# Output projection of a hybrid decoder layer as seven half-size products, its weight sums made by adding transfers

## The chip, the cores and the metric

One core of one Trainium2 chip. The metric is the device time of one execution of the whole layer in microseconds, as the median of several runs. TensorE (PE) does the matrix products, ScalarE (ACT) the casts and activations, VectorE (DVE) the elementwise work, GpSimd (POOL) a few scalings and a DMA queue of its own, SyncE (SP) the other DMA queue. Tiles live in SBUF, results of TensorE in banks of PSUM.

## The reference

One decoder layer in fp32 with batch 1, 512 tokens, D = 1024 and an FFN of width 2816. Three attention branches (sliding window, stick-breaking, cross-attention to a memory of 256 rows) are gated and merged; then:

```python
merged = (g[:, :, 0] * jnp.einsum('bse,ed->bsd', y_swa, w_branch_swa[l])
          + g[:, :, 1] * jnp.einsum('bse,ed->bsd', y_sb, w_branch_sb[l])
          + g[:, :, 2] * jnp.einsum('bse,ed->bsd', y_mem, w_branch_mem[l]))
mix = jnp.einsum('bsd,de->bse', merged, w_out[l])
h = h + rms_norm(mix, ln_mix_post[l])
u = rms_norm(h, ln_ffn_pre[l])
a = jax.nn.silu(jnp.einsum('bsd,df->bsf', u, w_gate[l])) * jnp.einsum('bsd,df->bsf', u, w_up[l])
ffn = jnp.einsum('bsf,fd->bsd', a, w_down[l])
h = h + rms_norm(ffn, ln_ffn_post[l])
```

The change is in `mix`: 512 x 1024 by 1024 x 1024.

## The kernel before

Every fp32 product is done as three products of fp32r parts (`mm3`, L167): high by high, high by low, low by high. `split` (L132) makes the parts: ScalarE casts the high part (L135), VectorE subtracts it from the source for the low part (L136). Weights come as 512 KB loads of 128 x 1024 on SyncE's queue and are split; activations are split where they are made.

Two streams (`Stream`, L33) lay out the work: `dn` runs the projections, gates and branches, `fs` the FFN. Each unit has a load, a split and its products; `run(us)` and `until(flag)` emit pieces of a stream, so that other code can be written in between. A stream's loads are emitted some units ahead of its products. Within an engine, instructions run in the order in which they stand; a framework sets the waits between engines. Blocks under `tc.high_priority()` may be moved up.

Buffers: `ckp` has 68 tiles of 128 x 512; `wp` holds the first stage's weights (`raw` 5, `hi` 4, `lo` 4 tiles of 128 x 1024) and is closed by `first.close()`; the FFN's pool `fp` is opened behind it in the same space, so that its first loads wait for whoever last read the space.

The last stages of `dn` are the gates of the MEM branch (`add_quarters`) and its four units of `branch` (L583): each product br is multiplied by its gate (L593), added to the sum of the other branches (L601), and the merged tile c (128 features x 512 tokens) is split into `mgh`, `mgl`. While the branch runs, eight loads of `w_out` and sixteen 512-wide splits are emitted (`out_load`, `out_split`).

`mix(t)` (L1051), for the four token tiles, does 2 output halves x 8 feature tiles x 3 products of 128 x 512 into two banks `mx`, 192 products in all. Then comes a chain of two norms: squares on ScalarE with a row sum (L1060), `rstd_small` (L1032: small operations, b and v, t and r, that go between VectorE and ScalarE), the gain (VectorE L1063), the residual `xr` (L1064), squares again (L1065), `rstd_small`, the gain (L1068) into the tiles `mt`. `turn(t)` (L1110) transposes `mt` on TensorE into `ut` (L1114) and makes the FFN's left factors: for t = 0, 1 the parts `B11`, `B21` (L1102, L1103) and copies `ur` (L1120); for t = 2, 3 `T1` and, later, `N2`, `N22`, `T3`, `T4`, from `ut` and `ur`. The FFN's products `gx`, `gw`, `gy` use these; gate, up and down are already done by seven products for eight, with weight sums of which some are made by adding transfers on GpSimd's queue (L1173). The first products of the program come behind nine warm-up products (`WARM`).

Of the kernel before, what the change touches and what calls it, by code (L numbers as in the profile page):

```python
# [103 lines left out]
def tile_kernel(ctx, tc, a):  # L104
# [913 lines left out]
    wo = {}  # L1018

    def out_load(h, q):  # L1020
        src = a["w_out"][:, h, 2 * q : 2 * q + 2].rearrange("p k n -> p (k n)")
        st[("wo", h, q)] = w_load(src, 1024)

    def out_split(h, q):
        raw = st.pop(("wo", h, q))
        for i in range(2):
            k = 2 * q + i
            wh, wl = ck(f"woh{h}{k}", F32R), ck(f"wol{h}{k}", F32R)
            split(raw[:, i * 512 : (i + 1) * 512], wh[:, :], wl[:, :])
            wo[(h, k)] = (wh[:, :], wl[:, :])  # L1030
# [380 lines left out]
    for i, (h, q) in enumerate(outs):
        out_load(h, q)
        out_split(h, q)
        dn.run(2.5)
# [188 lines left out]
```

## Time and profile before

| | |
|---|---|
| runs | 794.35, 794.44, 798.24 us |
| median | 794.44 us |
| profiled execution | 793.57 us, its span 791.8 us, granted clock 0.999 |

The profile is that of one execution. The page gives each engine's busy time as a share of the span, and the chain of work that ended last, followed back from the last instruction. The timeline of an engine has the start, the duration, engine, line, operation, output<-inputs, count, and in brackets the idle time before it with what ended it. The windows give each engine's busy time (and the number of its instructions) in stretches of the span, then TensorE's granted clock, the DMA engines' share and GB/s. Products are pipelined: 0.39 is how long one is in flight, and the distance of two starts is what one costs. Names are those of the program without buffer numbers.

### The profile page before, as it was taken

Reading aid. Unit: us, or ns where it says so; the run is one execution under the profiler, and the core shown is the slowest. Engines: PE = TensorE matmul, PEld = TensorE weight load, DVE = VectorE, ACT = ScalarE, POOL = GpSimd, SP = SyncE. Lnnn points to the kernel's source line nnn. Section 1 sums busy time; section 2 is a strip of 40 time slices with the busy share of each in tenths; the row PEclk is TensorE's granted clock in tenths of the full one; section 3 lists DMA queues with packets and bytes.
Section 4 is the critical chain, followed back from the end, with each engine's and each line's share of the span. In section 5 each row is a group of like instructions: output and inputs, shape, how many; then the busy total and the mean of one; then the engine's idle time right before and its main releaser. Section 6 shows DMA issues by size and latency. Waiting matters only on the chain.

```text
span 791.8 us, 12739 instructions
## 1 busy us (share of the span) xinstructions
PE 782.6 (99%) x4873; PEld 696.7 (88%) x4873; DVE 617.2 (78%) x960; ACT 454.8 (57%) x834; POOL 79.9 (10%) x103
## 2 busy tenths in 40 slices
PE   9999999999999999999999999999999999999996
PEld 6899887877888889889988899999999999888885
DVE  6998977754677796996694689868677767898797
ACT  7566755643664554765644477544445555666573
POOL 1101201000000001000013100010000000215200
PEclk9999999999999999999999999999999999999999
DMA  8443346122232308325769808877677751959802
GB/s 300 139 150 107 118 161 213 53 79 82 81 80 78 84 4 239 77 56 158 237 211 334 175 27 244 236 213 192 180 186 187 185 153 51 209 124 232 195 1 106
DMA packets 41870, 117.55 MB, mean 148 GB/s; under 512 B 4656, under 2 KB 6592, under 8 KB 41808
## 3 DMA queue, kind: packets, MB, share of 16 engines
q1 hardware_dynamic: 31872, 87.71, 34.1%
q0 software_dynamic: 9648, 28.82, 19.5%
q8 instruction: 38, 0.62, 0.3%
q14 instruction: 24, 0.20, 0.1%
q10 hardware_dynamic: 288, 0.20, 0.1%
HBM read 113.05 MB, written 3.67 MB: 147 GB/s over the span
## 4 chain that ended last, share of the span: by engine, by line
PE 95%; DVE 2%; issue 1%; DMA 0%; ACT 0%; SPq 0%; DVEq 0%
PE gx L172 5%; PE gx L169 5%; PE gx L171 5%; PE g L169 3%; PE br L169 3%; PE g L172 3%; PE br L171 3%; PE g L171 3%; PE br L172 3%; PE x L171 3%; PE x L172 3%; PE x L169 3%; PE gy L172 2%; PE gy L171 2%; PE gy L169 2%; PE mx L171 2%
## 5 line engine op out<-in xcount | busy, mean ns | idle before, releaser
L135 ACT CAST hi<-gw 128x1024 fp32r<-128x1024 f32 x77 | 79.8, 1048 | 81.7 <-DVE gw L1191 40.4
L136 DVE TENSOR_TENSOR lo<-gw,hi 128x1024 fp32r<-128x1024 f32 x77 | 93.6, 1223 | 34.0 <-ACT hi L135 33.9
L135 ACT CAST hi<-raw 128x1024 fp32r<-128x1024 f32 (+2 forms) x52 | 53.8, 1040 | 52.8 <-PE g L171 13.7
L136 DVE TENSOR_TENSOR lo<-raw,hi 128x1024 fp32r<-128x1024 f32 (+2 forms) x52 | 62.9, 1213 | 21.0 <-ACT hi L135 20.8
L1173 POOL DMA_DIRECT2D gw<-in_w_gu x27 | 23.3, 893 | 190.2 <-DMA gw<-in_w_gu 117.2
L135 ACT CAST hi<-r 128x1024 fp32r<-128x1024 f32 (+1 forms) x24 | 23.6, 982 | 19.9 <-PE y L172 5.3
L171 PE MATMUL x<-lo,lh 128*128 128x512 f32 x88 | 34.2, 389 | 0.0
L169 PE MATMUL x<-hi,lh 128*128 128x512 f32 x88 | 34.2, 389 | 0.0
L172 PE MATMUL x<-hi,ll 128*128 128x512 f32 x88 | 34.1, 389 | 0.0
L825 DVE TENSOR_TENSOR_SCAN p<-r,anew 128x512 f32<-128x512 f32 (+1 forms) x24 | 24.7, 1040 | 8.1 <-ACT r L189 7.6
L136 DVE TENSOR_TENSOR lo<-r,hi 128x1024 fp32r<-128x1024 f32 (+1 forms) x24 | 27.1, 1130 | 3.7 <-ACT hi L135 3.6
L136 DVE TENSOR_TENSOR lo<-qw,hi 128x1024 fp32r<-128x1024 f32 x18 | 21.9, 1219 | 8.9 <-ACT hi L135 8.9
L135 ACT CAST hi<-qw 128x1024 fp32r<-128x1024 f32 x18 | 18.9, 1050 | 15.8 <-PE g L171 3.7
L135 ACT CAST hi<-bp 128x512 fp32r<-128x512 f32 x33 | 19.1, 620 | 13.4 <-PE y L172 4.8
L136 DVE TENSOR_TENSOR lo<-bp,hi 128x512 fp32r<-128x512 f32 x33 | 22.2, 708 | 5.4 <-ACT hi L135 5.1
L172 PE MATMUL gx<-N2h,lo 128*128 128x256 f32 x88 | 25.0, 284 | 0.3 <-DVE lo L136 0.3
L169 PE MATMUL gx<-B11h,hi 128*128 128x256 f32 x88 | 25.1, 285 | 0.2 <-ACT B11h L1102 0.2
L172 PE MATMUL gw<-B21h,lo 128*128 128x256 f32 x88 | 25.0, 284 | 0.0
L169 PE MATMUL mx<-woh,mgh 128*128 128x512 f32 x64 | 25.0, 390 | 0.0
L171 PE MATMUL gx<-B11l,hi 128*128 128x256 f32 x88 | 25.0, 284 | 0.0
L172 PE MATMUL mx<-woh,mgl 128*128 128x512 f32 x64 | 24.9, 389 | 0.0
L172 PE MATMUL gy<-T1h,lo 128*128 128x256 f32 x88 | 24.9, 283 | 0.0
(910 smaller groups left out, 2900.8 us busy)
## 6 DMA issues: line engine op xcount, KB each, us to landing
gw<-in_w_gu SPq DMA_DIRECT2D x57, 512.0 KB, 5.0
gw<-in_w_gu POOLq DMA_DIRECT2D x27, 512.0 KB, 6.8
raw<-in_w_p SPq DMA_DIRECT2D x26, 512.0 KB, 4.2
qw<-in_w_p SPq DMA_DIRECT2D x15, 512.0 KB, 4.2
raw<-in_w_br SPq DMA_DIRECT2D x12, 512.0 KB, 3.8
bp<-in_w_dn SPq DMA_DIRECT2D x22, 256.0 KB, 8.4
r<-in_w_dn POOLq DMA_DIRECT2D x10, 512.0 KB, 8.2
raw<-in_w_out SPq DMA_DIRECT2D x8, 512.0 KB, 4.4
```

Of the source, the lines that this page charges most:

```text
L135: ins = nc.scalar.copy(hi, raw)
L136: lows = nc.vector.tensor_tensor(lo, raw, hi.bitcast(F32), op=ALU.subtract)
L169: one = nc.tensor.matmul(out, lh, rh, start=start, stop=False, skip_group_check=True)
L171: nc.tensor.matmul(out, *two, start=False, stop=False, skip_group_check=True)
L172: st["product"] = nc.tensor.matmul(out, *three, start=False, stop=stop, skip_group_check=True)
L825: ins = nc.vector.tensor_tensor_scan(p[:, :w], left1[i][:, :w], anew[:, o : o + w], 0.0, op0=ALU.mult, op1=ALU.max)
L1173: nc.gpsimd.dma_start(gw[(n, key)][:, :], g_src(n, i, j), accum_op=ALU.add)
```

## The change

`w_out` and `merged` are each seen as 2 x 2 blocks (feature half by output half; feature half by token half), and the product of blocks is done with seven half-size products p1 to p7 instead of eight. Each is 2 token tiles x 4 feature tiles x 3 products of 128 x 512: 168 products instead of 192.

- Weights: the sums of blocks of `w_out` are made in place: 12 plain loads of 256 KB (`wo_raw`, SyncE) and 16 transfers that add (`wo_plus`, GpSimd's queue), with 28 splits of 512 (`wo_split`). A tile is split for one product, then added to, then split for the next. The factors of p6 and p3 take four `hi`/`lo` pairs of `wp`.
- Left factors: made in the merged tiles in `branch` and in `turned_s`, `turned_r`, `turned_q`, `turned_d`, by 256-wide differences and sums and 256-wide splits.
- Results: p1, p5, p6 are copied from PSUM (ScalarE); p2, p3 and p7 are added to or subtracted from the copies (VectorE joins). `mix(0)` and `mix(1)` read such copies; `mix(2)` and `mix(3)` read the bank behind p4 and the join of p7. The norms of `mix` are as before, ten lines or so further down per line number (squares L1122 and L1127, gains L1125, residual L1126, L1130; turn's casts L1164, L1165, L1182, transposes L1176; FFN loads L1232, adding ones L1235).
- Places: the weights' loads start in the middle of the MEM gates (`dn.mark("half")`); `first.close()`, and with it `fp`, comes behind p3(1) instead of ahead of the first mix; `turn(0)` and `turn(1)` stand between the last products; `WARM` is 11.

```diff
-WARM = 9
+WARM = 11
...
-                h, l = ck(f"mgh{c}", F32R), ck(f"mgl{c}", F32R)
-                split(acc[:, :], h[:, :], l[:, :])
-                merged[c] = (h, l)
+                merged[c] = acc
+                if c < 4:
+                    if c % 2 == 0:
+                        ma.append((ck(f"mah{c}", F32R), ck(f"mal{c}", F32R)))
+                    sl = slice((c % 2) * 256, (c % 2) * 256 + 256)
+                    split(acc[:, :256], ma[-1][0][:, sl], ma[-1][1][:, sl])
+                    continue
+                mbd.append(parts(f"mbd{c}", acc))
+                nc.vector.tensor_tensor(acc[:, 256:], merged[c - 4][:, 256:], acc[:, 256:], op=ALU.subtract)
...
+    def wo_raw(key, j, h):
+        wsum[key] = [ck(f"wo{key}{k}") for k in range(4)]
+        for k, t in enumerate(wsum[key]):
+            nc.sync.dma_start(t[:, :], a["w_out"][:, h, 4 * j + k])
+
+    def wo_plus(key, j, h):
+        for k, t in enumerate(wsum[key]):
+            nc.gpsimd.dma_start(t[:, :], a["w_out"][:, h, 4 * j + k], accum_op=ALU.add)
...
+        if p not in ("p6", "p3"):
+            hl = tuple(ck(f"wo{p}{x}{k}", F32R)[:, :] for x in "hl")
+        else:
+            if k % 2 == 0:
+                uid[0] += 1
+                st["wo_two"] = [wp.tile([P, 1024], F32R, tag=x, name=f"{x}{uid[0]}", bufs=4) for x in ("hi", "lo")]
+            hl = tuple(x[:, (k % 2) * 512 : (k % 2) * 512 + 512] for x in st["wo_two"])
...
+    def turned_q(k):
+        lo, hi = merged[k], merged[4 + k]
+        nc.vector.tensor_tensor(hi[:, :256], lo[:, :256], hi[:, :256], op=ALU.add)
+        split(hi[:, :256], *(x[:, :256] for x in mqs[k]))
...
+    MIX = dict(p1="x", p6="x", p7="x", p4="x", p5="y", p3="y", p2="w")
...
+        with tc.high_priority():
+            if p in ("p1", "p5", "p6"):
+                t = mkeep[(p, i)] = ck(f"mk{p}{i}")
+                nc.scalar.copy(t[:, :], ps[:, :])
+            elif p == "p2":
+                t = mkeep[("p1", i)]
+                nc.vector.tensor_tensor(t[:, :], ps[:, :], t[:, :], op=ALU.add)
+            elif p == "p3":
+                t = mkeep[("p6", i)]
+                nc.vector.tensor_tensor(t[:, :], ps[:, :], t[:, :], op=ALU.subtract)
+            elif p == "p7":
+                t = mkeep[("p5", i)]
+                nc.vector.tensor_tensor(t[:, :], t[:, :], ps[:, :], op=ALU.subtract)
...
     def mix(t):
...
-            mm3(ps[h][:, :], (merged[k][0][:, tok], merged[k][1][:, tok]), wo[(h, k)], k == 0, k == KC - 1)
+        ps = (mkeep[("p1", i)], mkeep[("p6", i)]) if t < 2 else (mbank[("x", i)], mkeep[("p5", i)])
...
     dn.until(f"branch{MEM}")
+    for i in range(2):
+        mix_mm("p1", i)
...
+    mix_mm("p5", 0)
+    mix_mm("p6", 0)
+    for k in range(4):
+        wo_split("p7", "b", k)
+        turned_d(k)
+    mix_mm("p3", 0)
+    table("natural_log_exp_and_others")
+    tmp[0] = mix(0)
+    for k in range(4):
+        wo_split("p4", "r", k)
+    for p in ("p5", "p6", "p3"):
+        mix_mm(p, 1)
     first.close()
...
     fs.ahead(2, -1)
     tmp[1] = mix(1)
     fs.ahead(4, 0)
+    mix_mm("p7", 0)
+    turn(0, tmp[0])
+    mix_mm("p4", 0)
     tmp[2] = mix(2)
-    turn(0, tmp[0])
     fs.ahead(5, 3)
+    mix_mm("p7", 1)
+    turn(1, tmp[1])
+    mix_mm("p4", 1)
     tmp[3] = mix(3)
-    turn(1, tmp[1])
```

The order of the instructions at three places, before and after. First VectorE, around the first norm: `mkp60` is the kept copy of p6 for token tile 0, `mkp50` that of p5, `wop4l` are lows of p4's weights, `ssm0` the row sums of mix(0)'s squares, `mt0` and `xr0` its tiles. Before:

```order
L136 TENSOR_TENSOR mgl6_4366<-g16_2044,mgh6_4365 128x512
L136 TENSOR_TENSOR mgl7_4413<-g17_2077,mgh7_4412 128x512
L1036 TENSOR_SCALAR b_m0_4478<-ssm0_4472 128x1
L1038 SCALAR_TENSOR_TENSOR v_m0_4479<-ssm0_4472,b_m0_4478 128x1
L1040 SCALAR_TENSOR_TENSOR t_m0_4480<-r_m0_4481,v_m0_4479 128x1
L1041 SCALAR_TENSOR_TENSOR r_m0_4481<-t_m0_4480,r_m0_4481 128x1
L1063 SCALAR_TENSOR_TENSOR mt00_4474<-mx00_4422,r_m0_4481,bc_g_post0_4395 128x512
L1063 SCALAR_TENSOR_TENSOR mt01_4475<-mx01_4423,r_m0_4481,bc_g_post1_4396 128x512
L1064 TENSOR_TENSOR xr00_4379<-xr00_4379,mt00_4474 128x512
L1064 TENSOR_TENSOR xr01_4380<-xr01_4380,mt01_4475 128x512
```

And after:

```order
L136 TENSOR_TENSOR wop7l3_4608<-wob3_4193,wop7h3_4607 128x512
L1110 TENSOR_TENSOR mkp60_4587<-my0_4560,mkp60_4587 128x512
L1051 TENSOR_SCALAR b_m0_4633<-ssm0_4627 128x1
L1053 SCALAR_TENSOR_TENSOR v_m0_4634<-ssm0_4627,b_m0_4633 128x1
L136 TENSOR_TENSOR wop4l0_4662<-wor0_3921,wop4h0_4661 128x512
L136 TENSOR_TENSOR wop4l1_4666<-wor1_3922,wop4h1_4665 128x512
L1055 SCALAR_TENSOR_TENSOR t_m0_4635<-r_m0_4636,v_m0_4634 128x1
L136 TENSOR_TENSOR wop4l2_4670<-wor2_3923,wop4h2_4669 128x512
L1056 SCALAR_TENSOR_TENSOR r_m0_4636<-t_m0_4635,r_m0_4636 128x1
L136 TENSOR_TENSOR wop4l3_4674<-wor3_3924,wop4h3_4673 128x512
L1113 TENSOR_TENSOR mkp50_4573<-mkp50_4573,mx0_4418 128x512
L1125 SCALAR_TENSOR_TENSOR mt00_4629<-mkp10_4431,r_m0_4636,bc_g_post0_4306 128x512
```

Ahead of the first norm's small operations now stands a join, among them four weight lows, and behind them another join, which is of p7(0).

Second, ScalarE, around the squares of mix(2) and mix(3): `ut00` is the transposed tile of turn(0), `ut10` that of turn(1), `hi158` the high part of an FFN weight. Before, up to the squares of mix(3):

```order
L1060 ACTIVATE mt20_4673,ssm2_4671<-mx20_4621 128x512
L1060 ACTIVATE mt21_4674,ssm2_4671<-mx21_4622 128x512
L1102 CAST B11h0_3611<-ut00_4705 128x2x128
L189 ACTIVATE t_m2_4679<-ssm2_4671,b_m2_4677 128x1
L189 ACTIVATE r_m2_4680<-t_m2_4679 128x1
L1102 CAST B11h1_3613<-ut00_4705 128x2x128
L1065 ACTIVATE mt20_4673,ssh2_4672<-xr20_4387 128x512
L1065 ACTIVATE mt21_4674,ssh2_4672<-xr21_4388 128x512
L1120 COPY ur00_4715<-ut00_4705 128x512
L189 ACTIVATE t_h2_4695<-ssh2_4672,b_h2_4693 128x1
L1102 CAST B21h0_3615<-ut01_4706 128x2x128
L189 ACTIVATE r_h2_4696<-t_h2_4695 128x1
```

After, the squares of mix(2) and what stands ahead of them:

```order
L1164 CAST B21h1_3619<-ut01_4803 128x2x128
L1164 CAST B11h0_3613<-ut10_4896 128x2x128
L135 CAST hi158_4879<-gw152_4778 128x1024
L1182 COPY ur01_4813<-ut01_4803 128x512
L1122 ACTIVATE mt20_4838,ssm2_4836<-mx0_4418 128x512
L1122 ACTIVATE mt21_4839,ssm2_4836<-mkp50_4573 128x512
L1164 CAST B21h0_3617<-ut11_4897 128x2x128
L189 ACTIVATE t_m2_4844<-ssm2_4836,b_m2_4842 128x1
```

The squares of mix(2) stood ahead of turn(0)'s casts; now they stand behind the first of turn(1)'s and an FFN cast. And after, the squares of mix(3):

```order
L1182 COPY ur11_4907<-ut11_4897 128x512
L1127 ACTIVATE mt20_4838,ssh2_4837<-xr20_4496 128x512
L1127 ACTIVATE mt21_4839,ssh2_4837<-xr21_4497 128x512
L189 ACTIVATE t_h2_4860<-ssh2_4837,b_h2_4858 128x1
L189 ACTIVATE r_h2_4861<-t_h2_4860 128x1
L1122 ACTIVATE mt30_4932,ssm3_4930<-mx1_4433 128x512
L1122 ACTIVATE mt31_4933,ssm3_4930<-mkp51_4690 128x512
```

They stand behind `r_h2`, the end of mix(2)'s second norm, and behind all of turn(1)'s casts and copies. Before, they also stood behind `r_h2`, but ahead of all of turn(1)'s, with `B21h1` and `ur01` of turn(0) between.

Third, TensorE, from the last product of the mix to the first of the FFN: `ut10`, `ut11` are turn(1)'s transposes, `ut20` those of turn(2). Before:

```order
L169 MATMUL mx31_4741<-woh17_4356,mgh7_4412 128x512
L171 MATMUL mx31_4741<-wol17_4357,mgh7_4412 128x512
L172 MATMUL mx31_4741<-woh17_4356,mgl7_4413 128x512
L1114 MATMUL ut10_4824<-c_ident_364,mt10_4570 128x128 x4
L1114 MATMUL ut11_4825<-c_ident_364,mt11_4571 128x128 x4
L169 MATMUL gx0_4847<-B11h0_3611,hi159_4617 128x256
L1114 MATMUL ut20_4874<-c_ident_364,mt20_4673 128x128 x4
L171 MATMUL gx0_4847<-B11l0_3612,hi159_4617 128x256
```

And after:

```order
L169 MATMUL mx1_4433<-wop4h3_4673,mbd7h_4413 128x512
L171 MATMUL mx1_4433<-wop4l3_4674,mbd7h_4413 128x512
L172 MATMUL mx1_4433<-wop4h3_4673,mbd7l_4414 128x512
L1176 MATMUL ut10_4896<-c_ident_366,mt10_4738 128x128 x4
L1176 MATMUL ut11_4897<-c_ident_366,mt11_4739 128x128 x4
L169 MATMUL gx0_4965<-B11h0_3613,hi155_4785 128x256
L171 MATMUL gx0_4965<-B11l0_3614,hi155_4785 128x256
L172 MATMUL gx0_4965<-B11h0_3613,lo155_4786 128x256
```

Turn(1)'s transposes still follow the last product; turn(2)'s first stands later, behind more of the FFN's products.

More of the change, by code (lines that the diff above doesn't have):

```diff
@@ L579, in mem_vals @@
         return gen
-    merged = [None] * 8
+    merged, ma, mbd = [None] * 8, [], []
     def branch(b, c2, order):
@@ L634, in tile_kernel @@
             add_quarters(b, 0)
+            dn.mark("half")
             add_quarters(b, 1)
@@ L1016, in bcast, with wo_split @@
         return t
[L1018 to L1030, printed above, removed]
+    wsum, wt = {}, {}
+    def wo_raw(key, j, h):
[5 more added lines that the diff above has]
+            nc.gpsimd.dma_start(t[:, :], a["w_out"][:, h, 4 * j + k], accum_op=ALU.add)
+    def wo_split(p, key, k):
+        if p not in ("p6", "p3"):
[5 more added lines that the diff above has]
+            hl = tuple(x[:, (k % 2) * 512 : (k % 2) * 512 + 512] for x in st["wo_two"])
+        split(wsum[key][k][:, :], *hl)
+        wt[(p, k)] = hl
     def rstd_small(name, ss):
@@ L1049, in x_load, with turned_s, turned_r @@
             nc.sync.dma_start(hres[t][h][:, :], a["x"][t * P : (t + 1) * P, h * 512 : (h + 1) * 512])
+    mqs, mrd = [], []
+    mbank, mkeep = {}, {}
+    def turned_s(k):
+        mqs.append((ck(f"mqh{k}", F32R), ck(f"mql{k}", F32R)))
+        split(merged[4 + k][:, 256:], *(x[:, 256:] for x in mqs[k]))
+    def turned_r(k):
+        lo, hi = merged[k], merged[4 + k]
+        mrd.append((ck(f"mrh{k}", F32R), ck(f"mrl{k}", F32R)))
+        nc.vector.tensor_tensor(lo[:, 256:], lo[:, :256], lo[:, 256:], op=ALU.subtract)
+        nc.vector.tensor_tensor(lo[:, :256], hi[:, 256:], lo[:, :256], op=ALU.subtract)
+        split(lo[:, :256], *(x[:, :256] for x in mrd[k]))
@@ L1406, in down @@
         return gen
-    outs = [(h, q) for h in range(2) for q in range(4)]
-    dn.until(f"gates{MEM}")
[L1411 to L1414, printed above, removed]
+    dn.until("half")
+    wo_raw("r", 0, 0)
+    wo_raw("b2", 1, 0)
+    dn.run(4.0)
+    for k in range(4):
+        wo_split("p1", "r", k)
+        dn.run(2.0)
+    wo_plus("r", 0, 1)
+    dn.until(f"gates{MEM}")
+    wo_raw("b", 1, 1)
+    for k in range(4):
+        wo_split("p2", "b2", k)
+        dn.run(1.3)
+    for k in range(4):
+        wo_split("p5", "r", k)
+        dn.run(1.3)
+    wo_plus("r", 1, 1)
+    gpost = bcast("g_post")
+    gfpre = bcast("g_fpre")
+    for k in range(4):
+        wo_split("p3", "b", k)
+        dn.run(1.3)
+    wo_plus("b", 0, 1)
+    dn.until(f"branch{MEM}")
+    for i in range(2):
+        mix_mm("p1", i)
+    for k in range(4):
+        turned_s(k)
+    for k in range(4):
+        turned_r(k)
     for t in range(NT):
         x_load(t)
-    gpost = bcast("g_post")
-    gfpre = bcast("g_fpre")
-    dn.until(f"branch{MEM}")
+    for k in range(4):
+        wo_split("p6", "r", k)
+    wo_plus("r", 1, 0)
+    for i in range(2):
+        mix_mm("p2", i)
+    for k in range(4):
+        turned_q(k)
+    tmp = {}
+    mix_mm("p5", 0)
+    mix_mm("p6", 0)
+    for k in range(4):
+        wo_split("p7", "b", k)
[3 more added lines that the diff above has]
+    tmp[0] = mix(0)
+    for k in range(4):
+        wo_split("p4", "r", k)
+    for p in ("p5", "p6", "p3"):
+        mix_mm(p, 1)
     first.close()
```

20 lines of the change are left out of this document (14 added, 6 removed).

## The prediction

> **What bounds the kernel now.** I read the page first: the busy shares, then the chain that ended last.
>
> ```profile
> span 791.8 us, 12739 instructions
> PE 782.6 (99%) x4873; PEld 696.7 (88%) x4873; DVE 617.2 (78%) x960; ACT 454.8 (57%) x834; POOL 79.9 (10%) x103
> ...
> PE 95%; DVE 2%; issue 1%; DMA 0%; ACT 0%; SPq 0%; DVEq 0%
> ```
>
> TensorE is busy all the way and 95% of the last chain is its own work, so a product taken away is worth its full spacing as long as nothing else becomes late. The table of windows shows how much room the other engines have around the output projection: the branch stretch and the first half of the mix, the part of the mix in which VectorE had nothing to do, the norms, and the first FFN block.
>
> ```profile
> core 0: us, PE busy (x) PEld busy (x) DVE busy (x) ACT busy (x) POOL busy (x), PEclk, DMA share, GB/s
> 392.00:432.70 40.70, 40.70 (x181) 33.72 (x180) 29.64 (x52) 18.25 (x38) 9.12 (x7) 1.00 0.86 271
> 415.65:424.34 8.69, 8.69 (x40) 7.20 (x39) 0.00 (x0) 0.00 (x0) 5.05 (x6) 1.00 1.02 407
> 424.34:463.40 39.06, 38.89 (x210) 33.44 (x209) 28.37 (x69) 24.25 (x67) 6.02 (x7) 1.00 0.75 168
> 463.40:485.70 22.30, 22.00 (x185) 21.80 (x184) 21.47 (x38) 15.24 (x31) 1.72 (x2) 1.00 0.46 119
> ```
>
> VectorE is the second engine here: idle for 8.69 us, then 28.37 of 39.06, then 21.47 of 22.30, which is full. The TensorE timeline (start, duration) says how that last stretch meets the products.
>
> ```profile
> 410.31 0.39 PE L169 MATMUL mx<-woh,mgh 128*128 128x512 f32 x1
> ...
> 437.74 0.39 PE L171 MATMUL mx<-wol,mgh 128*128 128x512 f32 x1
> ...
> 484.62 0.39 PE L172 MATMUL gx<-N2h,lo 128*128 128x256 f32 x1 [0.30 <-DVE lo L136]
> ```
>
> At 484.62 TensorE waits 0.30 us for a VectorE subtract. So the norms, the turned blocks and this subtract form a VectorE chain that already ends exactly with TensorE: if that chain ends later, all of the program behind it moves by as much.
>
> **The change, part by part.** *The products.* 192 become 168. From 410.31 to 437.74 there are 121 spacings, 27.43 / 121 = 0.2267 us each (the 0.39 is a pipelined duration). 24 products less are 5.44 us of TensorE. They count only if the VectorE chain above ends 5.44 us earlier too.
>
> *The added work on VectorE and ScalarE.* The rows that price it:
>
> ```profile
> 401.44 0.68 DVE L136 TENSOR_TENSOR mgl<-g,mgh 128x512 fp32r<-128x512 f32 x1
> 402.05 0.68 DVE L136 TENSOR_TENSOR wol<-raw,woh 128x512 fp32r<-128x512 f32 x1
> ...
> 466.33 0.42 DVE L1201 TENSOR_TENSOR aq<-gp,sg 128x256 f32<-128x256 f32 x1
> 466.66 0.68 DVE L1123 TENSOR_TENSOR t<-ut,ur 128x512 f32<-128x512 f32 x1
> ...
> 483.35 2.35 DVE L136 TENSOR_TENSOR lo<-gw,hi 128x1024 fp32r<-128x1024 f32 x2
> ...
> 402.08 1.14 ACT L135 CAST woh<-raw 128x512 fp32r<-128x512 f32 x2
> ```
>
> By starts, a 512-wide operation costs VectorE 0.60 us, a 256-wide one 0.33 to 0.34, a 1024-wide one 1.14 (half of 2.35, less the overlap of neighbours). Weight lows: 28 for 16, +12 x 0.60 = 7.2. Lows and differences of the merged factors: 8 x 0.60 before, 4 x 0.60 and 36 x 0.34 now, +9.8. Six joins of half products, +3.6. Together +20.6 us on VectorE. ScalarE gets 12 more weight casts (0.57 each), 20 256-wide ones for four 512-wide, and six copies; at 0.57 for every one that is 34 x 0.57 = 19.4 us at most, and at 18.25 busy of 40.70 it has the room.
>
> Is VectorE late before the norms begin? The first norm, mix(0), now needs the join of p3(0), whose last product is the 98th in TensorE's new order: 410.31 + 97 x 0.2267 = 432.3, its result 0.4 later, 432.7. VectorE has, from the branch's first add at 392.4 up to that join, 41 operations of 0.60, 36 of 0.34 and one of 1.14, 38.0 us, in 40.3. It fits, with 2.3 us to spare. GpSimd takes from that:
>
> ```profile
> 412.32 1.70 DVE L136 TENSOR_TENSOR wol<-raw,woh 128x512 fp32r<-128x512 f32 x2
> 413.95 1.70 DVE L136 TENSOR_TENSOR mgl<-g,mgh 128x512 fp32r<-128x512 f32 x2
> ...
> 412.40 3.58 POOL L1015 TENSOR_SCALAR bc_g_post<-bc_g_post 128x512 f32<-128x512 f32 x2 [54.34 <-DMA bc_g_post<-in_g_post]
> ```
>
> While GpSimd scales the gains (1.79 us each), four 512-wide lows took 0.85 each. All four scalings now fall into the full stretch: 7.2 us of GpSimd at a VectorE slowed by 0.60/0.85 cost 2.1 us. That is just inside the 2.3, so I cost it at nothing; without cover it would be up to 2.1. The Trainium skill, "SBUF — State Buffer", section "SBUF: two separate sides", has it harder: a VectorE operation with two SBUF inputs and a GpSimd operation that reads SBUF take one port pair by an exclusive lock, and the loser fully blocks. By that rule VectorE would lose all 7.2 us and the sum below would be 4.9 us higher; the row, slowed and not blocked, decides.
>
> *The chain of norms.* Before, it runs as follows.
>
> ```profile
> 424.34 0.60 ACT L1060 ACTIVATE mt<-mx 128x512 f32<-128x512 f32 x1 [11.22 <-PE mx L172]
> ...
> 426.73 1.41 DVE L1063 SCALAR_TENSOR_TENSOR mt<-mx,r_m,bc_g_post 128x512 f32<-128x512 f32 x2
> 428.06 1.28 DVE L1064 TENSOR_TENSOR xr<-xr,mt 128x512 f32<-128x512 f32 x2
> ...
> 431.85 0.22 DVE L1040 SCALAR_TENSOR_TENSOR t_h<-r_h,v_h 128x1 f32<-128x1 f32 x1
> 432.10 0.16 DVE L1041 SCALAR_TENSOR_TENSOR r_h<-t_h,r_h 128x1 f32<-128x1 f32 x1
> ...
> 454.94 0.60 ACT L1060 ACTIVATE mt<-mx 128x512 f32<-128x512 f32 x1 [0.68 <-PE mx L172]
> ...
> 462.00 1.42 DVE L1068 SCALAR_TENSOR_TENSOR mt<-xr,r_h,bc_g_fpre 128x512 f32<-128x512 f32 x2
> 463.33 0.68 DVE L1123 TENSOR_TENSOR t<-ut,ur 128x512 f32<-128x512 f32 x1
> ```
>
> It starts at 424.34 and ends at 463.4; the last token tile alone takes 454.94 to 463.4, 8.5 us. After the change the first squares need the join: 432.7 + 0.68 = 433.4, so the chain starts **9.1 us later**. Does it run faster than before? I walked it in the new order of the engines. mix(0): 433.4 + 8.5, and in its row on VectorE stand four lows of p4 (2.4): 444.3. mix(1): squares at 442.4, then 8.5, two 1024-wide lows, the join of p7(1) and three 256-wide lows, 3.9: 454.8. Then TensorE's transposes of turn(1) from 454.4 (it waits about 3.2 us for them), and on ScalarE in its order B11h, a 1024-wide cast (hi158) and a copy; only behind these the squares of mix(2), at 456.75. ScalarE holds the squares of mix(3) until r_h2 is done, 456.75 + 7.2 = 463.95 (8.5 less the last pair, 1.33), although p4(1) ended long before. Then 8.5 more: the last mt at 472.5 instead of 463.4, again **+9.1**. From there VectorE's row is that of before, to the subtract at 483.35 with its zero slack, so the 484.62 moves by 9.1. The 5.44 us saved turn into waiting: TensorE stands about 14.5 us in all, most at ut10 (3.2), ut30 (2.7) and the blocks behind them.
>
> How little could it be? VectorE's work from the join to the last mt: four norms of 3.86 (1.33 + 1.20 + 1.33: the pairs above less their overlap of 0.08), some 5 of 32 small operations of 0.16 to 0.22, four p4 lows 2.4, three joins 1.8, four 1024-wide lows 4.56, eight 256-wide lows 2.7, together 32.5. Packed without a gap from 432.7 it ends at 465.2: **+1.8** is the least.
>
> *The transfers.* w_out is read in 28 transfers instead of 8, 16 of them adding ones on GpSimd's queue. p3's factors now lie where the FFN's load buffers go, so of the FFN's loads the second waits for the last product of p3(1), the 132nd, at 410.31 + 132 x 0.2267 = 440.2, and on SyncE's queue every later load stands behind it.
>
> ```profile
> 410.05 3.97 SPq L1170 DMA_DIRECT2D gw<-in_w_gu  x5
> ...
> 424.31 0.85 POOL L1173 DMA_DIRECT2D gw<-in_w_gu  x1 [0.37 <-issue]
> ...
> DMA to landing us min/median/max: 3.5/7.7/17.8
> ```
>
> Before, they were issued from 410.05. The seventh behind that wait is what hi158 reads, ahead of mix(2)'s squares: wanted at 455.3. At the 271 GB/s of the first window a 524 KB load takes 1.93: 440.2 + 3.5 + 6 x 1.93 = 455.3, no cost. Before, the fifth load had landed by 424.31 (the transfer issued there adds onto it), 14.3 after the first; two more make 18.1, so 458.3, +3. With three adding transfers in between it is 440.2 + 3.5 + 9 x 1.93 = 461, about +6. Adding transfers of this kind into weight sums of w_out are in no row here. I take **+2**, near the row of the fifth, and keep 0 and +6.
>
> *Two more warm-up products.*
>
> ```profile
> 1.35 3.85 PE L176 MATMUL warm<-idle 128*128 128x512 bf16 x9 [1.35 <-DVE idle L684]
> 4.88 0.55 PE L169 MATMUL kb<-uh,hi_first 128*128 128x512 f32 x1
> ...
> 6.00 0.40 PE L169 MATMUL kb<-uh,hi_first 128*128 128x512 f32 x1
> 6.24 0.39 PE L171 MATMUL kb<-uh,lo_first 128*128 128x512 f32 x1
> ...
> 7.92 0.50 PE L171 MATMUL kb<-uh,lo_first 128*128 128x512 f32 x1 [0.16 <-DVE lo_first L136]
> ```
>
> Nine take about 0.42 each, so two more are 0.84. The first three real products are slow (4.88 to 6.00, 0.37 each; 0.23 to 0.24 after), and would then run mostly fast: 0.43 back, and the wait of 0.16 at 7.92 covers the rest in part. **+0.25**, between 0 and 0.84; a gain is not there, since only 0.43 is to be had for 0.84.
>
> *Sum*, for the profiled execution of 793.57: 9.1 + 2 + 0.25 = 11.35, so 804.9. The median shown, 794.44, lies 0.87 above: **805.8 us**.
>
> **The rivals.** *Faster*: the saving reaches the end, 794.44 - 5.44 = 789.0, or less of it. The chain would have to end at 458 or before; VectorE's 32.5 us alone, from the 98th product, go to 465. For it speaks only that the new order differs, so that some of this work might be done earlier than I read. It decides if the last mt ends before 459. *VectorE packs*: the waits that I walked (behind B11h, hi158, r_h2) are filled by other VectorE work and the chain ends at 465 to 467: +1.8 to +3.7 and the warm-up, 796.5 to 798.4, no change. Against it: before, with the same kind of row, VectorE was busy 28.37 of 39.06, not 39. *The loads decide*: the loads held back to 440.2 arrive at 461 and set mix(2): +6 in place of +2, 809.8; the window of 407 GB/s, full at 1.02, shows that the transfers can fill. *The clock*: the products after a gap run slow. The start shows slow products, spaced 0.37 to 0.42, from 1.35 to 6.00, 4.65 us, then full speed. After each of the two gaps near 3 us that could cost 4.65 x (1 - 0.227/0.39) = 1.9, less what the chain hides: 808 to 810. The granted clock in all windows is 1.00, but they hold no such gap. The Trainium skill, "TensorE: Matmul & The Clock Gate", section "What's actually happening", says that an idle window of about 3.4 us halves the clock; by it, gaps of 3.2 and 2.7 stay mostly just short of it.
>
> **How the numbers follow.** The forecast (+6 to +10) gets 0.60: its start is given by a count of products, and its end by orders that are written down. VectorE packs 0.13, late loads 0.09, the clock 0.11, faster 0.07. About 0.5%, 4 us, is what a measurement of this kernel can tell from no change: faster 0.07, same 0.13, slower 0.60 + 0.09 + 0.11 = 0.80. The range goes from the least of VectorE, 796, to late loads with the warm-up's 0.84 and part of the clock's price, 812.
>
> **What would show it.** Right: mx rows from about 410 at the old spacing; the first square of mix(0) near 433; mix(2)'s squares behind a cast of gw, near 457; the last mt of mix(3) near 472; TensorE idle by 10 us or more between 437 and 495, put down to ACT B11h or to the mt rows; the second gw load issued near 440. Wrong: squares of mix(0) before 430, or the last mt before 460 (then it is faster); TensorE waiting already between 392 and 432 for mrl or mql (VectorE or GpSimd later than its row); a granted clock clearly below 1 in 440 to 500.

## The result and the profile after

| | before | after |
|---|---|---|
| median of 4 runs | 794.39 us | 802.99 us |
| lowest and highest | 793.83, 798.24 | 802.70, 804.67 |
| profiled execution | 793.57 us, span 791.8 | 802.70 us, span 800.9 |
| granted clock, mean | 0.999 | 0.992 |

The ratio is 1.0102, interval 1.0068 to 1.0137: slower by 8.6 us, where 11.4 was predicted. The page of the kernel after:

```profile
PE 783.4 (98%) x4851; PEld 696.5 (87%) x4851; DVE 637.8 (80%) x1010; ACT 467.5 (58%) x868; POOL 93.9 (12%) x119
...
PE 91%; DVE 4%; DMA 1%; ACT 1%; issue 1%; SPq 0%; DVEq 0%; ACTq 0%
```

TensorE's share of the last chain falls from 95% to 91% and VectorE's grows from 2% to 4%; VectorE has 20.6 us more to do (637.8 - 617.2), just the predicted sum. The windows are the same four stretches as before (the first starts 0.4 later, at the branch's first add).

```profile
392.40:432.70 40.30, 40.30 (x179) 33.38 (x178) 39.48 (x78) 22.74 (x49) 17.10 (x16) 1.00 0.74 161
415.65:424.34 8.69, 8.69 (x40) 7.21 (x39) 8.69 (x22) 4.61 (x14) 2.92 (x4) 1.00 0.92 274
424.34:463.40 39.06, 32.61 (x149) 26.75 (x148) 33.32 (x77) 25.66 (x67) 4.84 (x6) 0.91 0.75 211
463.40:485.70 22.30, 20.19 (x154) 19.57 (x153) 19.28 (x43) 14.95 (x38) 4.35 (x5) 0.92 0.88 177
```

VectorE, third of the busy columns, is full in the first two, where before it had 8.69 us with nothing to do. TensorE is still full there, so up to 432.70 the new work makes it wait for nothing. The loss is in the third window: TensorE 32.61 of 39.06 (38.89 before), and there the granted clock falls to 0.91. The timeline of ScalarE and VectorE shows the chain of norms: the join of p3(0), the first squares of the four tiles (of tile 0 the second square, which needs that join), what stands ahead of mix(2), and the end.

```profile
433.19 0.69 DVE L1110 TENSOR_TENSOR mkp<-my,mkp 128x512 f32<-128x512 f32 x1 [1.31 <-PE my L172]
433.91 0.63 ACT L1122 ACTIVATE mt<-mkp 128x512 f32<-128x512 f32 x1 [2.39 <-DVE mkp L1110]
...
442.63 0.61 ACT L1122 ACTIVATE mt<-mkp 128x512 f32<-128x512 f32 x1
...
454.99 0.37 ACT L1164 CAST B11h<-ut 128x256 fp32r<-128x256 f32 x1 [1.00 <-PE ut L1176]
455.65 1.04 ACT L135 CAST hi<-gw 128x1024 fp32r<-128x1024 f32 x1 [0.28 <-DMA gw<-in_w_gu]
456.60 0.58 ACT L1182 COPY ur<-ut 128x512 f32<-128x512 f32 x1
457.07 0.60 ACT L1122 ACTIVATE mt<-mx 128x512 f32<-128x512 f32 x1
...
463.96 0.58 ACT L1122 ACTIVATE mt<-mx 128x512 f32<-128x512 f32 x1
...
471.55 1.42 DVE L1130 SCALAR_TENSOR_TENSOR mt<-xr,r_h,bc_g_fpre 128x512 f32<-128x512 f32 x2
472.88 0.68 DVE L1185 TENSOR_TENSOR t<-ut,ur 128x512 f32<-128x512 f32 x1
```

And TensorE's, with what it waits for:

```profile
410.77 0.39 PE L169 MATMUL mx<-wop1h,mah 128*128 128x512 f32 x1
...
448.51 0.50 PE L169 MATMUL mx<-wop4h,mbd4h 128*128 128x512 f32 x1 [0.82 <-DVE mkp L1113]
454.30 1.32 PE L1176 MATMUL ut<-c_ident,mt 128*128 128x128 f32 x8 [2.75 <-DVE mt L1130]
458.40 0.58 PE L171 MATMUL gx<-B11l,hi 128*128 128x256 f32 x1 [2.60 <-DVE B11l L1165]
...
472.35 1.32 PE L1176 MATMUL ut<-c_ident,mt 128*128 128x128 f32 x8 [2.10 <-DVE mt L1130]
...
493.99 0.39 PE L172 MATMUL gx<-N2h,lo 128*128 128x256 f32 x1 [0.29 <-DVE lo L136]
```

The products saved became waits for VectorE. The two largest, with 1.50 us of work between them, stand about the transposes of tile 1. The last row answers to 484.62 before: TensorE waits there as it did (0.29 and 0.30), 9.37 us later, and the profiled executions differ by 802.70 - 793.57 = 9.13.

The first product of the output projection does not come at the same time in each execution (410.31 to 412.20 in the profiled ones). So the kernels are compared below by the time since that product: its row is subtracted. "t" is the first subtract into t behind the last norm (463.33 before, 472.88 after); for tile 0 the second square stands.

| kernel | mix(0) | mix(1) | mix(2) | mix(3) | t | median, us |
|---|---|---|---|---|---|---|
| before | 14.62 | 20.76 | 31.48 | 43.26 | 53.02 | 794.39 |
| after | 23.14 | 31.86 | 46.30 | 53.19 | 62.11 | 802.99 |
| before_late | 21.96 | 28.92 | 36.23 | 44.27 | 53.26 | 794.46 |
| pair | 23.14 | 31.86 | 45.95 | 47.14 | 59.50 | 800.64 |
| tok0 | 22.13 | 29.97 | 42.39 | 51.50 | 60.44 | 800.93 |
| mix2early | 23.14 | 31.86 | 42.68 | 53.48 | 62.29 | 802.90 |
| tok0early | 22.13 | 29.97 | 38.91 | 48.98 | 57.70 | 798.42 |
| tok0pair | 22.13 | 29.97 | 42.38 | 43.57 | 58.55 | 802.59 |
| nolow | 22.30 | 28.76 | 41.37 | 49.49 | 57.60 | 798.46 |

After's t comes 62.11 - 53.02 = 9.09 later than before's: the whole difference arises in this stretch.

### The profile page after: what moved, and what is told of

It reads as the page before. It is cut to its first block, busy times and chain, and to the rows that moved or that the text cites. A ratio compares the mean times of both kernels' runs of the same rounds, so it can differ in the third digit from the quotient of the medians.

```text
span 800.9 us, 12837 instructions
## 1 busy us (share of the span) xinstructions
PE 783.4 (98%) x4851; PEld 696.5 (87%) x4851; DVE 637.8 (80%) x1010; ACT 467.5 (58%) x868; POOL 93.9 (12%) x119
## 3 DMA queue, kind: packets, MB, share of 16 engines
HBM read 116.19 MB, written 3.67 MB: 150 GB/s over the span
## 4 chain that ended last, share of the span: by engine, by line
PE 91%; DVE 4%; DMA 1%; ACT 1%; issue 1%; SPq 0%; DVEq 0%; ACTq 0%
PE gx L172 5%; PE gx L169 5%; PE gx L171 5%; PE g L169 3%; PE g L172 3%; PE br L171 3%; PE br L169 3%; PE g L171 3%; PE br L172 3%; PE x L169 2%; PE x L172 2%; PE x L171 2%; PE gy L172 2%; PE gy L171 2%; PE gy L169 2%; PE qx L169 1%
## 5 line engine op out<-in xcount | busy, mean ns | idle before, releaser
L1235 POOL DMA_DIRECT2D gw<-in_w_gu x27 | 23.3, 897 | 193.5 <-DMA gw<-in_w_gu 103.6
L172 PE MATMUL gx<-B11h,lo 128*128 128x256 f32 x88 | 26.4, 300 | 0.0
L169 PE MATMUL gw<-B21h,hi 128*128 128x256 f32 x88 | 25.0, 285 | 0.0
```

The source lines that it names most:

```text
L169: one = nc.tensor.matmul(out, lh, rh, start=start, stop=False, skip_group_check=True)
L172: st["product"] = nc.tensor.matmul(out, *three, start=False, stop=stop, skip_group_check=True)
L1235: nc.gpsimd.dma_start(gw[(n, key)][:, :], g_src(n, i, j), accum_op=ALU.add)
```

## The experiments

The theory that I took from the prediction: the chain starts late, and the order in which the engines stand (mix(2) behind turn(1)) keeps it late. Its rivals: the late loads, the clock gate, the warm-up, and the amount of VectorE's work whatever its order. The ratios are to runs of the kernel before that were timed beside each experiment (medians 794.02 to 794.38 us).

**p3own: the buffers of p3's factors.** Of the FFN's loads only those behind p3(1) can be late; here p3 has tiles of its own.

```diff
-        if p not in ("p6", "p3"):
+        if p != "p6":
```

> The changed kernel with p3's weight factors in tiles of their own, so that the FFN's loads no longer wait for p3(1)'s last product at 440.2. Theory (the norms decide, the loads come just in time): the second load is issued some 15 us earlier, ScalarE's 0.28 us wait ahead of hi158 goes, and the time falls by 0.3 us at most. Rival, the loads held back decide: the time falls by 2 us or more, to 801.

803.23 us (803.07 to 803.57), ratio 1.0114 [1.0101, 1.0128]: no gain. SyncE's loads behind the first one, in after and then in p3own:

```profile
440.89 7.32 SPq L1232 DMA_DIRECT2D gw<-in_w_gu  x10
```

```profile
436.22 3.77 SPq L1232 DMA_DIRECT2D gw<-in_w_gu  x8
```

The second load leaves 4.67 us earlier, not 15: it now waits for a product of an `mx` bank, and p6, whose factors stayed in `wp`, writes one. ScalarE in p3own:

```profile
449.97 1.05 ACT L135 CAST hi<-gw 128x1024 fp32r<-128x1024 f32 x1 [1.16 <-DMA gw<-in_w_gu]
...
457.22 0.60 ACT L1122 ACTIVATE mt<-mx 128x512 f32<-128x512 f32 x1
```

A cast waits 1.16 us for its load at 449.97, and mix(2)'s squares still come where they came (457.22, 46.47 behind the first product). The edit moved more than the loads: the first two 1024-wide lows now stand within mix(0)'s norm (440.98 and 443.38), so mix(1)'s squares come 2.01 us later than after's and the stretch behind them is 1.84 shorter. Loads that leave 4.67 us earlier bring nothing; what loads without any wait would bring, this run does not show. In after itself the wait that they cause ahead of mix(2) is 0.28 us.

**warm9: the warm-up.**

```diff
-WARM = 11
+WARM = 9
```

> The changed kernel with nine warm-up products instead of eleven. Theory: p1's first product comes 0.46 us earlier, at 410.31 as before the change, and the chain and the end with it: 0.3 to 0.5 us less, 802.5. Rival (the start is covered by later waits): no difference, within 0.1 us.

803.17 us (802.71 to 806.78), ratio 1.0126 [1.0108, 1.0144]: no difference; the expected gain of half a microsecond is not there. The first products of warm9 on TensorE:

```profile
6.45 0.59 PE L169 MATMUL kb<-uh,hi_first 128*128 128x512 f32 x1
6.87 0.40 PE L171 MATMUL kb<-uh,lo_first 128*128 128x512 f32 x1
```

Full speed comes at 6.87 here, at 6.00 in the profile before, both with nine warm-up products. In these two profiles the moment does not follow from their number. The first product of the output projection comes at 410.70 here and at 410.77 in after, so the two products more are not why it is later than 410.31.

**keepwarm: the clock gate.** After the waits of 2.75 and 2.60 us the granted clock was 0.58 and lower, after the one of 2.10 it was 0.71. Windows of the kernel after:

```profile
456.00:460.00 4.00, 1.60 (x7) 1.60 (x8) 3.45 (x10) 3.92 (x12) 0.00 (x0) 0.58 1.04 271
460.00:464.00 4.00, 4.00 (x23) 4.00 (x22) 3.01 (x8) 2.44 (x9) 1.75 (x2) 0.57 1.07 296
464.00:468.00 4.00, 4.00 (x36) 4.00 (x36) 3.27 (x10) 1.74 (x7) 1.75 (x2) 1.00 1.06 214
...
472.00:476.00 4.00, 3.64 (x19) 3.23 (x20) 4.00 (x8) 3.30 (x7) 1.75 (x2) 0.71 0.79 128
```

keepwarm puts 21 products without use into the gaps about the transposes of tile 1; in its text turn(1) stands behind p4(1), and the order of products, fillers and transposes on TensorE is fixed.

```diff
+        if t == 1:
+            last = fill(11, last)
...
+        if t == 1:
+            st["filled"] = fill(10, last)
```

> The changed kernel with 21 products without use (11 ahead of turn(1)'s transposes, 10 behind them) in the two gaps of 2.75 and 2.60 us, so that TensorE does not stand still there; ScalarE's and VectorE's order is that of the changed kernel. Theory (the slow products behind the gaps are hidden, since the norms end later anyway): the granted clock between 456 and 463 goes from 0.58 to 1.0, TensorE waits that much longer at ut30, the time stays at 803 within 0.5 us. Rival (the slow clock is part of the loss): 2 to 3.6 us less, about 800.

804.36 us (803.57 to 804.93), ratio 1.012 [1.0092, 1.0148]. One window and the end of the chain in keepwarm:

```profile
460.00:464.00 4.00, 4.00 (x35) 3.98 (x34) 3.72 (x9) 2.42 (x7) 1.75 (x2) 1.00 1.05 293
```

```profile
473.23 1.69 PE L1188 MATMUL ut<-c_ident,mt 128*128 128x128 f32 x8 [2.76 <-DVE mt L1130]
```

The clock is full, 35 products fit where 23 did, and TensorE waits 2.76 us for the last norm in place of 2.10. The t comes 62.14 behind the first product, after's 62.11, and the squares of the four tiles within 0.03 us of after's. So the slow clock is there and costs nothing here: VectorE is the later one. The median is 1.4 above after's; in its profile the output projection starts 0.85 later (411.62), and where the rest is from I did not find out.

**before_late: only the late start.** The kernel before, with the last six of tile 0's 48 products put behind all of tile 1's. No work is added.

```diff
+    mix_mm(0, ((0, 6, 0), (0, 6, 1), (6, 8, 0)))
+    mix_mm(1)
+    mix_mm(0, ((6, 8, 1),))
```

> The kernel before, its eight-product output projection kept, with the products of token tiles 0 and 1 interleaved so that the last product that the first norm needs is the 96th (as late as in the changed kernel); no work added on any engine. The first squares' second half comes at about 432.3 instead of 424.9. If a late start of the chain is by itself what costs, the end moves by 7 to 9 us, to about 802. If the chain of before had room (VectorE stood 10.7 us idle in it, and the last norm's squares waited for TensorE's last product), the four norms catch up with that last product and the time rises by 0 to 2 us, to 794 to 796. I expect the second.

794.46 us (794.02 to 796.39), ratio 1.0002 [0.999, 1.0013]: no change. Its timeline:

```profile
412.20 0.39 PE L169 MATMUL mx<-woh,mgh 128*128 128x512 f32 x1
...
434.16 0.60 ACT L1070 ACTIVATE mt<-mx 128x512 f32<-128x512 f32 x1 [5.35 <-PE mx L172]
441.12 0.58 ACT L1070 ACTIVATE mt<-mx 128x512 f32<-128x512 f32 x1
...
448.43 0.58 ACT L1070 ACTIVATE mt<-mx 128x512 f32<-128x512 f32 x1
...
456.47 0.60 ACT L1070 ACTIVATE mt<-mx 128x512 f32<-128x512 f32 x1
...
465.46 0.68 DVE L1133 TENSOR_TENSOR t<-ut,ur 128x512 f32<-128x512 f32 x1
```

The chain begins at 21.96, that is 7.34 later than before, and t moves by 0.24. In the kernel before each tile's squares were released again by TensorE (454.94 for mix(3), "0.68 <-PE mx"); its early start was slack. This is shown for the kernel before, whose VectorE has room; no run moves the start of the changed kernel alone. Here the four norms run one behind the other, 7 to 8 us apart. After's start lies only 1.18 behind this one. By the table after loses 7.13 us between mix(1)'s and mix(2)'s squares (14.44 for 7.31) and 1.76 between mix(0)'s and mix(1)'s (8.72 for 6.96), and gains back 1.15 before mix(3)'s.

**pair: the norms of tiles 2 and 3 side by side.** Their operations alternate, and turn(1) comes behind both.

```diff
-    turn(0, tmp[0])
     mix_mm("p4", 0)
-    tmp[2] = mix(2)
-    fs.ahead(5, 3)
+    turn(0, tmp[0])
     mix_mm("p7", 1)
-    turn(1, tmp[1])
     mix_mm("p4", 1)
-    tmp[3] = mix(3)
+    tmp[2], tmp[3] = mix_two((2, 3))
+    fs.ahead(5, 3)
+    turn(1, tmp[1])
```

> The changed kernel with the norms of the last two token tiles written side by side, so that the squares of mix(3) stand right behind those of mix(2) on ScalarE instead of behind r_h2. Same work on every engine. Theory (the norms stand in series): the squares of mix(2) stay near 457.1, the last mt comes at about 468.8 instead of 473.0, TensorE's wait at ut30 (2.10 us) shrinks and the time falls by 3 to 4 us, to about 799.5. Rival, VectorE's added work as such (20 us more on it): the same work remains, so the time stays within 1 us of 803.

800.64 us (799.86 to 801.50), ratio 1.0081 [1.0068, 1.0095]: 2.35 of the 3.5 expected. mix(3)'s squares come 6.05 us earlier and t 2.61; two norms share VectorE and each takes longer.

**tok0: p1 and p2 of tile 0 first.** Both stand ahead of tile 1's.

```diff
-    for i in range(2):
-        mix_mm("p1", i)
+    mix_mm("p1", 0)
...
-    for i in range(2):
-        mix_mm("p2", i)
+    mix_mm("p2", 0)
+    mix_mm("p1", 1)
+    mix_mm("p2", 1)
```

> The changed kernel with the products of p1 and p2 written token tile 0 first; the scheduler then puts p3(0) nine products earlier (the 89th is its last) and the join of p7(0) behind the first norm's gains. Theory (the chain of norms starts with the join of p3(0)): that join starts 1.3 to 2.0 us earlier than 433.2, and the whole chain with it, as far as the FFN's loads let it: the squares of mix(2) near 455.5 and the time 1.5 to 2 us lower, about 801.2. Rival, VectorE is full ahead of the join: the join does not come earlier and the time stays at 803.

800.93 us (800.50 to 801.04), ratio 1.0084 [1.007, 1.0098]: the time as expected, the way not. The start is only 1.01 earlier (1.3 to 2.0 expected), yet mix(2)'s squares come 3.91 earlier, of which 2.22 are given back by mix(3)'s.

**best4 and pooldiff: both edits, and work for GpSimd.** best4 is tok0 and pair, with the join of p7 no longer moved up; pooldiff makes the 16 differences of factors on GpSimd as well.

```diff
-        with tc.high_priority():
+        with tc.high_priority() if p != "p7" else ExitStack():
```

```diff
-        nc.vector.tensor_tensor(lo[:, 256:], lo[:, :256], lo[:, 256:], op=ALU.subtract)
+        nc.gpsimd.tensor_tensor(lo[:, 256:], lo[:, :256], lo[:, 256:], op=ALU.subtract)
...
-        nc.vector.tensor_tensor(hi[:, :256], lo[:, :256], hi[:, :256], op=ALU.add)
+        nc.gpsimd.tensor_tensor(hi[:, :256], lo[:, :256], hi[:, :256], op=ALU.add)
```

> The changed kernel with three edits of order together: p1 and p2 token tile 0 first, the join of p7 without its priority, the norms of mix(2) and mix(3) side by side. Same work on every engine. Theory (order loses part, VectorE's added work the rest): the parts add, 2.1 + 2.3 + 0.5, so 798.1 and not below 795, since VectorE needs 32.5 us from the join of p3(0) to the last mt; slower than the kernel before. Rival (order alone is at fault): 794 or less.

> The same kernel as best4 with the sixteen 256-wide sums and differences of the merged factors (16 x 0.34 = 5.4 us of VectorE) on GpSimd. Theory (VectorE's amount of work is the rest of the loss): the join of p3(0) comes at TensorE's pace, about 1 us earlier, and the time falls by about 1 us against best4. Rival (GpSimd is slow and slows VectorE beside it): the factors come late, TensorE waits between 412 and 432, and the time is 1 to 5 us higher than that of best4.

best4: 804.33 us (803.06 to 807.83), ratio 1.0124 [1.0091, 1.0157], 6 above the expectation. What TensorE waited for in best4 between 405 and 500:

```profile
PE gx L171 <- DVE B11l L1192: 5.3, 2, 4.7
PE mx L169 <- DVE mkp L1113: 2.8, 1, 2.8
```

p4(1) uses the bank that the join of p7 reads; with the join late TensorE stands 2.8 us, and 4.7 us for a B11l. pooldiff: 813.79 us (812.96 to 813.93), ratio 1.0234 [1.0211, 1.0257]. GpSimd's groups between 404 and 450, and TensorE's row behind them:

```profile
L610 POOL TENSOR_TENSOR g<-g,g 128x256 f32<-128x256 f32 x4 | 4.9, 1215 | 0.0
...
L1082 POOL TENSOR_TENSOR g<-g,g 128x256 f32<-128x256 f32 x4 | 3.6, 906 | 0.3
```

```profile
433.79 0.80 PE L169 MATMUL mx<-hi,mrh 128*128 128x512 f32 x1 [3.33 <-ACT mrh L135]
```

An operation that VectorE does in 0.34 takes GpSimd 0.9 to 1.2 us, and now TensorE waits for a factor, ahead of any norm. So this run does not tell what relieving VectorE ahead of the join is worth; nolow, below, does.

**mix2early and tok0early: the old order.** mix2early undoes the change's order alone: mix(2) and mix(3) ahead of turn(0) and turn(1). tok0early is the same on tok0.

```diff
-    turn(0, tmp[0])
     mix_mm("p4", 0)
     tmp[2] = mix(2)
+    turn(0, tmp[0])
...
-    turn(1, tmp[1])
     mix_mm("p4", 1)
     tmp[3] = mix(3)
+    turn(1, tmp[1])
```

> The written order of before is put back around the norms: mix(2) ahead of the transposition of mix(0)'s result, mix(3) ahead of that of mix(1)'s, so that mix(2)'s two Squares stand on ScalarE ahead of B11h, hi158 and ur01 (in after behind them). Theory one (the order is what loses the 7 us between mix(1)'s and mix(2)'s squares: 14.44 us in after, 7.31 in the kernel before with a late join): mix(2)'s squares near 450 in place of 457.07, the last mt some 5 to 7 us earlier, 796 to 798 us. Theory two (VectorE is full there, and what mix(2) gains the transposition of tiles 0 and 1 gives back: 33.32 us of 39.06 busy in after): mix(2)'s squares come earlier but PE then waits for ut00, ut10 and B11l longer than the 0, 2.75 and 2.60 us of after, so that the last mt moves by no more than 2.5 us: 800 to 803 us. By walking the order out row by row I get some 2 us, so I lean to theory two: 801.

> The edit of tok0 (both p1 and p2 of token tile 0 ahead of those of tile 1, which gave 800.93) with the order of mix2early. If the two are independent, the gains add: 802.99 - 2.06 - whatever mix2early gains. If VectorE's amount of work is the floor (18.5 us free between 392.4 and 463.4 in before, 20.6 added), it stays above 795 whatever the order; theory one gives 794.5 to 796, theory two 798.5 to 801. I lean to 799.

mix2early: 802.90 us (802.60 to 804.07), ratio 1.0113 [1.0098, 1.0128], no gain. The timeline of mix2early:

```profile
454.61 0.57 ACT L1122 ACTIVATE mt<-mx 128x512 f32<-128x512 f32 x1
...
465.41 0.60 ACT L1122 ACTIVATE mt<-mx 128x512 f32<-128x512 f32 x1
```

```profile
457.04 1.97 PE L1176 MATMUL ut<-c_ident,mt 128*128 128x128 f32 x8 [4.39 <-DVE mt L1130]
```

mix(2)'s squares do come earlier, at 42.68 for 46.30. But the norm of tile 1 ends later, TensorE waits 4.39 us for its transposes where it waited 2.75, and the blocks of tiles 0 and 1 now lie between mix(2) and mix(3): 10.80 us for 6.89. What the order gave, it took back. The granted clock is 0.50 from 456 to 468 here and the eight transposes take 1.97 us for 1.32; how much of what was taken back is the clock's, the run does not separate. On tok0 the same order does help: tok0early takes 798.42 us (798.20 to 798.56), ratio 1.0054 [1.0038, 1.0071], 4.6 less than after. Its transposes of tile 1 and the window:

```profile
451.89 1.04 PE L1176 MATMUL ut<-c_ident,mt 128*128 128x128 f32 x8
```

```profile
424.34:463.40 39.06, 32.75 (x154) 27.15 (x153) 35.97 (x86) 28.30 (x75) 6.28 (x8) 0.92 0.85 247
```

No wait at the transposes, and VectorE is busy 35.97 of 39.06 in place of 33.32: more of its work is done in time.

**tok0pair: both edits, with the join kept at priority.**

> The edits of tok0 and of pair together, with the join of p7 kept at priority (best4 had both without it, and PE waited 4.74 us for B11l there). If the two gains are of different waits they add: 802.99 - 2.06 - 2.35 = 798.6. If both end at the same limit (VectorE's last row from B21l on), no more than the better one: 800.5. I lean to 798.8; below 795 would contradict the count of VectorE's work.

802.59 us (802.11 to 803.84), ratio 1.0109 [1.0094, 1.0124]: a miss by 3.8. The first t comes 3.56 earlier than after's, but that no longer is the end. Windows, then the timeline, of tok0pair:

```profile
456.00:460.00 4.00, 3.42 (x14) 2.44 (x13) 3.33 (x12) 3.07 (x11) 0.00 (x0) 0.50 1.05 273
460.00:464.00 4.00, 1.88 (x9) 1.58 (x8) 4.00 (x9) 1.33 (x4) 1.75 (x2) 0.50 1.06 289
464.00:468.00 4.00, 2.94 (x13) 2.94 (x14) 3.26 (x13) 3.90 (x11) 1.75 (x2) 0.50 1.06 210
```

```profile
465.06 0.58 PE L171 MATMUL gx<-B11l,hi 128*128 128x256 f32 x1 [3.18 <-DVE B11l L1192]
...
475.66 0.69 DVE L1212 TENSOR_TENSOR t<-ut,ur 128x512 f32<-128x512 f32 x1 [1.72 <-PE ut L1203]
```

The norms pushed the blocks of tile 1 back: TensorE waits 3.18 us for a B11l, works at half the clock until 468, and at 475.66 VectorE waits for TensorE. The clock's price, hidden in after, now lies on the path: the 17 products behind that wait, spaced 0.21 instead of 0.12, are 1.6 us of it. The rest of the miss I did not take apart.

**nolow: VectorE without the 28 weight lows.** Each product reads the high part twice; the low parts of w_out's sums are left out.

```diff
-        split(wsum[key][k][:, :], *hl)
-        wt[(p, k)] = hl
+        nc.scalar.copy(hl[0], wsum[key][k][:, :])
+        wt[(p, k)] = (hl[0], hl[0])
```

> This kernel leaves out the 28 low parts of the seven products' weight sums (each product reads the high part in the low part's place; PE's work is the same), so VectorE has 28 subtractions less, 16.8 us at the 0.60 us that one adds to a run of them, of which four (2.7 us) stand behind the join. Theory one (the amount of VectorE's work makes the change slow): with 17 of the 20.6 added microseconds gone the time falls under the kernel before, to 789 to 795. Theory two (the order makes it slow: the join of tile 0 waits for PE's product p7, not for VectorE, and mix(2) stands behind the transposition of tile 1 whatever VectorE has to do; only the four subtractions behind the join are on the path): the first norm's squares stay 23 us behind the first product of the output projection, the norm of tile 1 comes 1.8 to 2.7 us earlier and nothing else: 800 to 801.5. I lean to theory two.

798.46 us (797.99 to 802.19), ratio 1.0066 [1.004, 1.0092]: between the two theories, and outside both. The join and t of nolow on VectorE:

```profile
432.15 0.69 DVE L1110 TENSOR_TENSOR mkp<-my,mkp 128x512 f32<-128x512 f32 x1 [7.92 <-PE my L172]
...
468.17 0.68 DVE L1185 TENSOR_TENSOR t<-ut,ur 128x512 f32<-128x512 f32 x1
```

VectorE stands idle 7.92 us before the join, and the norms begin only 0.84 earlier: the start hangs on TensorE's order. t comes 4.51 earlier: 0.84 at the start, 2.26 between mix(0) and mix(1), where p4's lows were, 1.83 between mix(1) and mix(2), 0.81 at the end, and 1.23 lost between mix(2) and mix(3). Yet t is still 4.58 later than before's. The stretch that decides runs from the second square of mix(0) to t. Its windows in before_late, after and nolow, in this order:

```profile
434.16:465.46 31.30, 30.91 (x174) 26.81 (x173) 25.48 (x65) 21.25 (x63) 5.19 (x6) 1.00 0.68 138
```

```profile
433.91:472.88 38.97, 30.42 (x167) 25.92 (x165) 32.25 (x76) 25.99 (x71) 6.07 (x7) 0.91 0.83 226
```

```profile
432.87:468.17 35.30, 30.21 (x165) 25.47 (x164) 29.43 (x72) 26.24 (x71) 6.04 (x7) 0.95 0.82 228
```

After has 6.77 us more for VectorE to do there than before_late (32.25 for 25.48): four lows of p4, three joins, and two 1024-wide lows of FFN weights, which in before_late stand ahead of that square (427.89). The stretch is 7.67 longer, and VectorE is idle in it for 6.72 instead of 5.82. With the start, 1.18 later, this is the whole 8.85 us between the two t. nolow takes 2.82 us of work out of this stretch, and the stretch is 3.67 shorter; the 24 other lows stood ahead of it, where 7.92 us are now idle. Whether the two FFN lows would fill that time, if their loads came earlier, no run tried. The order of the instructions, which a scheduler writes, shifted too, so the shares of the stages are not exact.

**What follows.** No single edit carries the loss. By the windows above most of it is VectorE's additional work behind the first squares, which finds no idle time there. That is a comparison of traces; no run moves this work alone. Half of the loss goes when VectorE has 17 us less to do, or, with the work kept, when tile 0's p1 and p2 come first and mix(2) and mix(3) stand ahead of the turns. The order of the norms alone, the earlier loads and the warm-up brought nothing, and the clock costs nothing until TensorE is the later one. An estimate from these rows: without any idle time of VectorE after's t would come 23.14 + 32.25 = 55.39 behind the first product, 2.37 later than before's, so order alone, with this start and this work, does not reach the kernel before. Whether the two halves add I did not try; and no version tried beats the kernel before (the best, tok0early, is 0.54% over it).

## Why the prediction was right, and where not

- *24 products of 0.2267, 5.44 us, come to nothing.* Right in that nothing is gained: they turned into the waits of 0.82, 2.75, 2.60 and 2.10 us. Their size was off: TensorE was to stand about 14.5 us, 10 or more of them between 437 and 495, and is idle for 9.16 us there (busy 48.84 of 58.00). Of the rest about 2.1 us are the 23 slow products, 0.21 apart instead of 0.12; what remains I did not take apart.
- *VectorE +20.6 us, and just in time for the join.* Right: 20.6 by the pages, and the join waits 1.31 us for TensorE. GpSimd's four scalings took VectorE nothing that reached the path.
- *The start, +9.1.* Right as a row: 433.91 for 433.4. Wrong as a reason. "The chain starts 9.1 us later" and "the last mt ... again +9.1" read as if the late start was carried through. before_late shows that 7.34 us of late start alone cost 0.24 of t and nothing of the time: the chain before had slack, seen in its squares that TensorE released one tile after the other. Against before_late only 1.18 of the 8.85 us are the start's. That start and end are late by the same amount is chance.
- *The walk through the rows.* Right within 0.7 us: mix(1) 442.63 for 442.4, ut10 454.30 for 454.4, mix(2) 457.07 for 456.75, mix(3) 463.96 for 463.95, end of the last mt 472.97 for 472.5. This walk, not the start, held the cause: VectorE's row behind the join, and of it most the stretch from mix(1) to mix(2).
- *Mix(2) behind turn(1) as the place.* The place is right, but it is not a cause that can be undone by itself: mix2early takes the order away and gains nothing (on tok0 the same edit gains 2.51 us). What stands in the row is work that has to be done before the end, and in the other order it delays mix(3).
- *Late loads, +2.* The mis-sized term: hi158 waited 0.28 us, and in p3own loads 4.67 us earlier brought nothing. The load was wanted at 455.3 and was there at 455.65, by the first of the three sums (no cost).
- *Warm-up, +0.25.* Nothing measurable; warm9 has 803.17 for 802.99. Without these two terms the sum would be 794.44 + 9.1 = 803.5, and 802.99 was measured.
- *The rival of the clock.* Its mechanism occurred, and with it one of the signs of being wrong, a granted clock clearly below 1; its price did not: gaps of 2.75 and 2.60 us, 1.5 us of work between them, brought the granted clock to 0.57 for some 5 us, and one of 2.10 to 0.71, where the prediction had gaps of 3.2 and 2.7 pass. The Trainium skill, "TensorE: Matmul & The Clock Gate", section "What's actually happening", speaks of an idle window of about 3.4 us; these rows, with shorter gaps, do not agree with that. keepwarm shows that after hides it, tok0pair that it need not stay hidden.
- *VectorE packs.* Did not happen (33.32 of 39.06). With another order (tok0early, 35.97) it goes part of the way, to 798.42, where the rival had 796.5 to 798.4. Its 32.5 us of work were read well, though the terms as listed add up to 31.9: from the join to t VectorE is busy for 32.97 us.
